# Where VectorE's low parts, two weight sums and the reloads of late sums stand in the projections of a hybrid attention step

## Chip, cores and metric

The kernel runs on one core of a Trainium2 chip. The metric is the device time of one execution in microseconds (us). Before the change the median of three runs is 974.46 us (973.89 to 976.30). Five engines work from queues of their own: TensorE (PE in the profile; PEld are its weight loads), VectorE (DVE), ScalarE (ACT), GpSimd (POOL) and SyncE (SP), which only issues transfers.

## The reference, cut to what matters

One layer of a streaming encoder: RMS norm of x (1024 prompt rows and 64 sample rows, 1024 columns), one projection to 6144 columns, two attention branches (stick-breaking and chunk-band), a merge and an output projection.

```python
def project(x, norm_w, w_in, q_norm_w, k_norm_w):
    h = rms_norm(x, norm_w) @ w_in
    sb_q, sb_k, sb_v, sb_z, cb_q, cb_k, cb_v, cb_z, g_sb, g_cb = jnp.split(h, SPLIT_POINTS, axis=-1)
    ...
    cb_q = rms_norm(cb_q.reshape(lead + (N_HEADS_CB, HEAD_DIM)), q_norm_w)
    cb_k = rms_norm(cb_k.reshape(lead + (N_HEADS_CB, HEAD_DIM)), k_norm_w)
```

The change touches only the first quarter of the execution: the norm of x, and the projections to `cb_q`, `cb_k` and the two value blocks `sb_v` (columns 1024 to 1535) and `cb_v` (3072 to 3583).

## The kernel before

**High and low parts.** All operands are 32-bit floats. TensorE takes them in a reduced format, so each operand is split into a high part (a ScalarE copy that rounds) and a low part (the operand less its high part, one subtraction on VectorE or GpSimd). A product is three matmuls: high by high, low by high, high by low. For x the parts are `xhl`, for weights `whi`/`wlo` (from pool `wpool`) and `whix`/`wlox` (from `natx`), two buffers each. The low part's subtraction reads the high part, so it waits for ScalarE.

**Stage one, steps 0 to 223.** The row blocks of x are normed while the first two weight blocks are already multiplied. `early(at)` is called before each matmul and does the work listed for that step: `prep_s` (L302: square and row sum on ScalarE, then two small GpSimd operations), `prep_a` (L311: scaling on VectorE, at the steps in `SCALE`), `prep_b` (L321 to L330: eight transposes on TensorE, high part on ScalarE, low part on VectorE, at the steps in `READY`), and `W.split` (L134 high, L141 low) of the next weights. The row blocks come in the order `QO`: 0, 1, 2, 3, 8 (the sample rows), 4, 5, 6, 7.

**Passes over `cb_q` and `cb_k`.** For each of the blocks i = 2 to 5 nine row blocks (`ti` 0 to 8) are multiplied (L560), their head norms are taken (`evac_nat` L373 to L376 with two GpSimd operations, `norm_nat` L385), and three or four tiles later they are transposed and stored (`post_nat`: L408 on TensorE, L412 ScalarE, L413 VectorE, then stores). Between the tiles `make_t` builds sums of x: four combinations t0 to t3 of four slices each, in a hand-written order of `yield`s. t0 and t1 are made in these passes, and each slice of t1's unsplit sum is stored to DRAM (`d_t1`).

**The value products.** `sb_v` (j = 0) and `cb_v` (j = 1) are computed by a scheme that trades multiplications for sums: seven products of quarters, numbered s = 0 to 6, instead of eight. Their order is `ORDER`: (0,1), (0,2), (0,6), (0,0), (1,2), (1,1), (1,6), (0,4), (1,0), (1,4), (1,5), (0,5). The position in that list is q, and (q, n) with n = 0 to 3 is one quarter of a product: `part((q, n))` issues the other engines' work, then follow twelve matmuls (L820). Products with s = 0 are two short groups of sample rows only (L710). The weights are quarters of 512 rows and 256 columns, `quad[j, h, w]` (`load_quad`, L510), sums of them (`sum_w`, L440, kept in `made`), and their splits (`split_quad`: L518 high part, L519 low part). Product (0,4) needs all of t2, products (1,5) and (0,5) all of t3. Every second quarter an eviction (`evac_p`) adds a PSUM bank to a sum in SBUF: L726 for partial sums, L729 for a finished block, which `put_v` then stores. Banks are named in `BANKS`: (0,4) writes bank 3 after (1,2), whose result is read at the eviction of (1,1); (1,5) goes on adding to the banks of (1,4) once their eviction has read them.

**Late sums of x.** The second half of `make_t` makes t2 and t3, one slice per call at the quarters in `TJ`: reload the slice of `d_t1` (L211), two VectorE operations (L220, L221 for t2; L223, L224 for t3), then the split `put_t` (L175 high, L176 low), all in one go. The reload of the next slice is issued when a slice is begun; the tiles `d` have two buffers.

**What sets the order.** Each engine takes its instructions in the order in which this program issues them; the order is written out by hand (`manual_schedule`), and a helper adds the semaphore waits that the data needs. Nearly all transfers are issued by SP, in one queue, so a transfer that waits for a buffer holds those behind it.

Of the kernel before, what the change touches and what calls it, by code (L numbers as in the profile page):

```python
# [27 lines left out]
HF = T // 2  # L28
# [6 lines left out]
def hybrid_step_kernel(ctx: ExitStack, tc: tile.TileContext, x_prompt, x_sample, c_sbk, c_sbv, c_cbk, c_cbv,  # L35
# [141 lines left out]

    def make_t(tm, pool):
# [28 lines left out]
        got = {}  # L207

        def fetch(n, k):
            got[n, k] = pool.tile([128, HF], F32, name="d")  # L210
            SP.dma_start(got[n, k], d_t1[k])  # L211

        fetch(*late[0])
        yield
        for e, (n, k) in enumerate(late):
            d = got[n, k]
            if e < 7:
                fetch(*late[e + 1])
# [6 lines left out]
            put_t([t(n, s, k) for s in range(2)], d)  # L225
            yield

    psF = ctx.enter_context(tc.tile_pool(name="af", bufs=2, space=PS))
    with ExitStack() as ph:
# [275 lines left out]
        quad, comb, made = {}, {}, {}  # L505
# [6 lines left out]
        def split_quad(q, src, eng=None):  # L512
# [6 lines left out]
            (eng or G).tensor_tensor(out=l, in0=src, in1=h.bitcast(F32), op=OP.subtract)  # L519
# [42 lines left out]
        SCALE = [24, 48, 72, 96, 122, 148, 174]  # L562
        READY = [12, 36, 60, 84, 110, 136, 162, 190]

        def early(at):
# [60 lines left out]
        for i in range(2, nb):  # L626
# [4 lines left out]
            for ti, t in enumerate(TO):  # L631
# [56 lines left out]
        psB = nu = rw = ws = None  # L688
# [29 lines left out]
        TJ = [(0, 2), (1, 1), (2, 3), (4, 2), (5, 0), (6, 2), (7, 0), (7, 3), (9, 0)]  # L718
        BANKS = {0: "2", 2: "1", 4: "3", 5: "2", 6: "1", 7: "3", 9: "2"}
        u, banks = {(0, "2"): s1t[0]}, {}  # L720
# [11 lines left out]
        def part(at):  # L732
            nonlocal psB, nu, rw, ws, raw1
            if at[0] == 0:
                post_nat(*pend.pop(0))
            if at == (0, 0):
                split_quad(3, quad[0, 0, 1])
# [3 lines left out]
            elif at == (0, 2):  # L741
                sum_w(quad[0, 1, 0], quad[0, 1, 0], made[2], OP.subtract)
                u[0, "3"] = pn.tile([128, 4, 256], F32, name="made2", bufs=1)
# [1148 lines left out]
```

## Time and profile before

| What | Value |
|---|---|
| Median of three runs | 974.46 us (973.89 to 976.30) |
| The profiled execution | 975.09 us |
| Its span, first to last instruction | 973.2 us |
| TensorE busy | 950.6 us, 98% |
| VectorE busy | 595.6 us, 61% |
| ScalarE busy | 498.7 us, 51% |
| GpSimd busy | 382.4 us, 39% |
| Mean granted TensorE clock | 0.993 of full speed |
| Stage one / passes over q and k / value products | 10 to 51 us / 51 to 157 us / 157 to 234 us |

Rows of the order of time read: start in us from the span's start, duration in us, engine, line, operation, output tile <- input tiles, sizes, count, and in brackets the engine's idle time just before and what ended it. Rows of the waits read: engine, tile and line that waited <- the operation waited for, total us, times, longest. A wait for several things is put down to the one that came last in the profile.

### The profile page before, as it was taken

To read this page: it belongs to the slowest core of one execution; us is meant where nothing else is said; L and a number is where in the kernel's file an instruction comes from. 1 tells how busy PE (TensorE), PEld (TensorE's weight loads), DVE (VectorE), ACT (ScalarE), POOL (GpSimd) and SP (SyncE) were. 2 spreads that over 40 slices of the span, in tenths; PEclk is the share of its full clock that TensorE was granted. 3 is DMA by queue.
4 is the path that set the end of the run, shared out by engine and by line. 5 is a ranking of instruction groups with operands and counts; after the bars stand their busy time and mean duration, and the time that the engine had idled before them with its cause. 6 is when DMAs were issued, how large, how long until landed. Compare 5 with 4: busy or idle time off the path is not lost.

```text
span 973.2 us, 20499 instructions
## 1 busy us (share of the span) xinstructions
PE 950.6 (98%) x7547; PEld 903.8 (93%) x7547; DVE 595.6 (61%) x1172; ACT 498.7 (51%) x1151; POOL 382.4 (39%) x387
## 2 busy tenths in 40 slices
PE   8899999959999999999999999999999999999998
PEld 8899999959999999999999987878888888999998
DVE  6746866773554564543332197778678765499735
ACT  7656776222434433433332276667787775466220
POOL 3156664003644465665542201002331111586641
PEclk9999999979999999999999999999999999999999
DMA  7638666455556555565432997779699942862632
GB/s 257 212 128 294 216 241 229 162 165 185 171 178 183 157 166 183 164 192 165 140 116 80 269 259 195 182 202 248 208 297 263 244 126 76 250 204 69 219 126 87
DMA packets 177705, 182.78 MB, mean 188 GB/s; under 512 B 30713, under 2 KB 160125, under 8 KB 177478
## 3 DMA queue, kind: packets, MB, share of 16 engines
q1 hardware_dynamic: 166182, 166.60, 57.3%
q10 hardware_dynamic: 8608, 8.20, 2.6%
q0 software_dynamic: 2816, 6.69, 2.2%
q8 instruction: 60, 0.98, 0.4%
q14 instruction: 39, 0.32, 0.1%
HBM read 117.79 MB, written 63.64 MB: 186 GB/s over the span
## 4 chain that ended last, share of the span: by engine, by line
PE 71%; DMA 3%; ACT 2%; DVE 2%; issue 1%; SPq 1%; ACTq 0%; DVEq 0%
PE b L952 30%; PE o L1474 7%; PE z L1377 7%; PE pt L1430 7%; PE b L1799 6%; PE acc L1228 5%; PE b L1270 5%; PE acc L1121 2%; PE b L820 1%; DMA sq<-d_qsbT 1%; DMA ks<-d_ksbT 1%; PE acc L1842 1%; DVE acc L1315 0%; DMA d<-d_t 0%; PE acc L878 0%
## 5 line engine op out<-in xcount | busy, mean ns | idle before, releaser
L1430 PE MATMUL pt<-ident,be 128*128 128x128 f32 (+1 forms) x568 | 87.1, 277 | 0.9 <-ACT wT L1439 0.6
L1399 DVE TENSOR_TENSOR_SCAN be<-be,imp 128x128 f32<-128x128 f32 (+7 forms) x64 | 82.7, 1341 | 8.3 <-ACT be L1380 8.3
L1377 PE MATMUL z<-ks,sq 128*128 128x320 f32 (+5 forms) x384 | 87.7, 338 | 0.0
L1439 ACT ACTIVATE wT<-pt 128x512 f32<-128x512 f32 (+3 forms) x123 | 57.2, 498 | 44.0 <-PE pt L1430 43.9
L1430 PEld LDWEIGHTS pt<-ident,be 128*128 128x128 f32 (+1 forms) x568 | 66.2, 140 | 13.7 <-issue 5.1
L952 PE MATMUL b<-xm,wlox 128*128 128x256 f32 (+1 forms) x336 | 76.0, 286 | 0.0
L960 DVE TENSOR_TENSOR u<-b,s 128x256 f32<-128x256 f32 (+1 forms) x56 | 24.1, 439 | 70.6 <-PE b L952 68.7
L1377 PEld LDWEIGHTS z<-ks,sq 128*128 128x128 f32 x384 | 63.5, 190 | 2.2 <-ACT be L1380 0.9
L1474 PE MATMUL o<-wT,vp 128*64 128x256 f32 (+1 forms) x608 | 64.2, 357 | 0.0
L1474 PEld LDWEIGHTS o<-wT,vp 128*64 128x64 f32 x608 | 40.3, 137 | 22.4 <-issue 5.4
L952 PEld LDWEIGHTS b<-xm,wlox 128*128 128x128 f32 x336 | 56.8, 188 | 0.0
L1402 ACT ACTIVATE be<-be,sm 128x640 f32<-128x640 f32 (+5 forms) x68 | 47.2, 694 | 17.8 <-DVE sm L1401 17.5
L500 POOL TENSOR_TENSOR whix<-ws,whix 128x512 fp32r<-128x512 f32 x28 | 36.9, 1319 | 36.3 <-ACT whix L499 32.7
L1025 POOL DMA_DIRECT2D d_osb<-zt x20 | 10.8, 541 | 100.8 <-DVE zt L1488 49.2
L1380 ACT ACTIVATE be<-z 128x384 f32<-128x384 f32 (+6 forms) x104 | 48.2, 521 | 3.4 <-PE z L1377 2.9
L500 POOL TENSOR_TENSOR wlo<-ws,wlo 128x512 fp32r<-128x512 f32 x28 | 39.4, 1406 | 26.3 <-ACT wlo L499 24.7
L1390 ACT ACTIVATE be<-be,sm 128x640 f32<-128x640 f32 (+5 forms) x68 | 47.3, 695 | 3.8 <-DVE sm L1382 3.3
L1270 PE MATMUL b<-og,whi 128*128 128x384 f32 (+1 forms) x192 | 46.7, 327 | 0.0
L854 ACT ACTIVATE hl<-u 128x256 f32<-128x256 f32 (+1 forms) x40 | 16.9, 432 | 55.8 <-DVE u L972 17.7
L952 PE MATMUL b<-t0h,whix 128*128 128x256 f32 (+1 forms) x224 | 44.7, 289 | 0.0
L952 PE MATMUL b<-t3h,whi 128*128 128x256 f32 (+1 forms) x224 | 44.6, 289 | 0.0
L385 ACT ACTIVATE qn<-qn,rsn 128x64 f32<-128x64 f32 (+1 forms) x144 | 38.2, 339 | 11.3 <-POOL rsn L293 10.6
(440 smaller groups left out, 3304.6 us busy)
## 6 DMA issues: line engine op xcount, KB each, us to landing
wraw<-in_w_in_dram SPq DMA_DIRECT2D x34, 512.0 KB, 4.6
wrawx<-in_w_in_dram SPq DMA_DIRECT2D x16, 512.0 KB, 3.9
sq<-d_qsbT SPq DMA_DIRECT2D x32, 192.0 KB, 4.8
sq<-d_qcbT SPq DMA_DIRECT2D x32, 192.0 KB, 5.0
xt<-in_x_prompt_dram SPq DMA_DIRECT2D x8, 512.0 KB, 4.7
d_kcbT<-hl SPq DMA_DIRECT2D x8, 512.0 KB
d_qcbT<-hl SPq DMA_DIRECT2D x8, 512.0 KB, 5.0
d_ksbT<-hl SPq DMA_DIRECT2D x16, 256.0 KB, 3.2
```

The source lines that it names most:

```text
L500: G.tensor_tensor(out=t[:, 1], in0=src, in1=t[:, 0].bitcast(F32), op=OP.subtract)
L952: TE.matmul(ps[:, :m], w[:, hl_, k], right[s](x)[:, k, a:b], start=s < 3 and k == 0 and e == 0, stop=k == 3 and e == 2, skip_group_check=s ...
L1228: TE.matmul(ps[:, :e - a], w[:, p, cw], g[:, a:e], start=m % 12 == 0, stop=m % 12 == 11)
L1270: TE.matmul(pp[uu][:, :n], w[:, p, uu * 128:uu * 128 + 128], g[:, a:e], start=p == 0 and m == 0, stop=p == NPAIR - 1 and m == 2)
L1377: TE.matmul(z[:, :m], s[:, e, q0:q0 + 128], ks[:, h, o + x:o + y], start=(e, h) == parts[0], stop=(e, h) == parts[-1])
L1380: A.activation(be[:r, x:y], z[:r, :m], AF.Sigmoid, scale=-0.125)
L1390: A.activation(be[:, :n], be[:, :n], AF.Exp, bias=kp[:, j:j + 1], scale=-1.0, accum_out=kp[:, 2:3])
L1399: V.tensor_tensor_scan(be[:r, n - 1::-1], be[:r, n - 1::-1], im[:, ::-1], 0.0, op0=OP.mult, op1=OP.max)
L1430: TE.transpose(pt[:kr, x, :r], be[:r, kb * 128:kb * 128 + kr], ident[:r, :r])
L1439: A.activation(w[:, sl:sl + m, q0:q0 + r], pt[:, :m, :r], AF.Copy)
L1474: TE.matmul(o[hd * 64:hd * 64 + 64, c0:c1], vv[:kr, kb, hd * 64:hd * 64 + 64], wT[b, p, j, hd, s // 4][:kr, s % 4, c0:c1] if j < 4 else wT ...
L1799: TE.matmul(ps[:, t], left[s](xs_, k)[:, ts_], wt_[:, k], start=s < 3 and t == k == e == 0, stop=k == 3 and e == 2, skip_group_check=s > 2 ...
```

## The change

It has four parts.

1. Low parts. `split_quad` and the late sums no longer issue the low part's subtraction directly behind the high part. They append it to a list `lows`, which `put_lows` empties at the start of the next quarter product (in the last pass: after the next tile's norm). Quads 0 and 3 stay on GpSimd; quad 11's low part goes from GpSimd to VectorE.
2. Weight sums. The sums of `quad[0,0,0]` and of `quad[0,1,0]` move from quarters (0,3) and (0,2) into the last pass, to `ti` 6 and 8; for that `quad[0,1,0]` is loaded earlier, into the buffer where `quad[1,1,1]` was, and that one later. Several sums and splits in the later quarters move by one quarter.
3. Late sums of x. The first two reloads are issued together at quarter (0,1); the first slice's two VectorE operations run at (0,3), its split at (1,0). From (1,2) on two more buffers (`dl`, in a new pool `nd`) take reloads, so a reload is issued two slices ahead or more. The quarters in `TJ` are new.
4. Stage one. Two squares (`prep_s`) go from steps 60 and 84 to 66 and 92, one scaling from step 96 to 86, and the splits of weight block 2 from steps 166 and 200 to 178 and 202.

```diff
+    lows = []
+
+    def put_lows():
+        while lows:
+            eng, lo, src, hi = lows.pop(0)
+            eng.tensor_tensor(out=lo, in0=src, in1=hi.bitcast(F32), op=OP.subtract)
...
-        fetch(*late[0])
-        yield
+        fetch()
+        fetch()
+        nu = yield
         for e, (n, k) in enumerate(late):
-            d = got[n, k]
-            if e < 7:
-                fetch(*late[e + 1])
+            d = got[e]
+            if nu and len(got) < 4:
+                fetch(nu, "dl")
+                fetch(nu, "dl")
+            elif nu and len(got) < 8:
+                fetch(*((nu, "dl") if len(got) > 5 else ()))
...
-            put_t([t(n, s, k) for s in range(2)], d)
-            yield
+            if e == 0:
+                nu = yield
+            hi, lo = (t(n, s, k) for s in range(2))
+            A.activation(hi, d, AF.Copy)
+            lows.append((V, lo, d, hi))
+            nu = yield
...
-        def split_quad(q, src, eng=None):
+        def split_quad(q, src, eng=V):
...
-            (eng or G).tensor_tensor(out=l, in0=src, in1=h.bitcast(F32), op=OP.subtract)
+            lows.append((eng, l, src, h))
...
-        SCALE = [24, 48, 72, 96, 122, 148, 174]
+        SCALE = [24, 48, 72, 86, 122, 148, 174]
...
-                if p + 2 < 9:
+                if p + 2 < 9 and p not in (3, 4):
                     prep_s(QO[p + 2])
+            elif at in (66, 92):
+                prep_s(QO[5 + at // 92])
...
-            elif at == 166:
+            elif at == 178:
                 W.split((2, 0), V)
...
-            elif at == 200:
+            elif at == 202:
                 W.split((2, 1), V)
...
+                put_lows()
                 if (i, ti) == (nb - 1, 2):
...
-                    load_quad(1, 1, 1, wpool, "wraw", 2)
+                    load_quad(0, 1, 0, wpool, "wraw", 2)
...
-                    split_quad(0, made[2])
+                    split_quad(0, made[2], G)
+                if (i, ti) == (nb - 1, 6):
+                    sum_w(quad[0, 0, 0], quad[0, 0, 0], quad[0, 0, 1], OP.subtract)
                 if (i, ti) == (nb - 1, 7):
-                    split_quad(1, made[1], V)
-                    load_quad(0, 1, 0, pn, "made1", 1)
+                    split_quad(1, made[1])
+                if (i, ti) == (nb - 1, 8):
+                    load_quad(1, 1, 1, pn, "made1", 1)
+                    sum_w(quad[0, 1, 0], quad[0, 1, 0], made[2], OP.subtract)
...
-        TJ = [(0, 2), (1, 1), (2, 3), (4, 2), (5, 0), (6, 2), (7, 0), (7, 3), (9, 0)]
+        TJ = [(0, 1), (0, 3), (1, 0), (1, 2), (2, 3), (4, 2), (6, 2), (7, 0), (7, 2), (9, 0)]
...
         def part(at):
+            put_lows()
...
             elif at == (0, 2):
-                sum_w(quad[0, 1, 0], quad[0, 1, 0], made[2], OP.subtract)
...
-            elif at == (0, 3):
-                sum_w(quad[0, 0, 0], quad[0, 0, 0], quad[0, 0, 1], OP.subtract)
                 load_quad(1, 0, 1, wpool, "wraw", 2)
+                split_quad(2, quad[0, 1, 0])
...
-                split_quad(2, quad[0, 1, 0], V)
-            elif at == (1, 2):
+            elif at == (1, 1):
...
+                nd = ndx.enter_context(tc.tile_pool(name="nd", bufs=2))
+                for n in "23":
+                    u[1, n] = nd.tile([128, 4, 256], F32, name="u" + n, bufs=1)
...
             if at in TJ:
-                next(tjobs)
+                tjobs.send(nd)
```

More of the change, by code (lines that the diff above doesn't have):

```diff
@@ L206, in make_t, with fetch @@
         late = [(n, k) for n in (2, 3) for k in range(4)]
[L207 to L211, printed above, removed]
-        fetch(*late[0])
-        yield
-        for e, (n, k) in enumerate(late):
-            d = got[n, k]
-            if e < 7:
-                fetch(*late[e + 1])
+        got = []
+        def fetch(ds=None, name="d"):
+            got.append((ds or pool).tile([128, HF], F32, name=name, bufs=2))
+            SP.dma_start(got[-1], d_t1[late[len(got) - 1][1]])
+        fetch()
+        fetch()
+        nu = yield
+        for e, (n, k) in enumerate(late):
+            d = got[e]
[4 more added lines that the diff above has]
+                fetch(*((nu, "dl") if len(got) > 5 else ()))
             if n == 2:
@@ L503, in prep @@
                 load_raw(2 * i + 4)
-        quad, comb, made = {}, {}, {}
+        quad, comb, made, u = {}, {}, {}, {}
         def load_quad(j, h, w, pool, name, bufs):
@@ L666, in hybrid_step_kernel @@
                 if (i, ti) == (nb - 1, 5):
-                    split_quad(0, made[2])
+                    split_quad(0, made[2], G)
+                if (i, ti) == (nb - 1, 6):
+                    sum_w(quad[0, 0, 0], quad[0, 0, 0], quad[0, 0, 1], OP.subtract)
                 if (i, ti) == (nb - 1, 7):
-                    split_quad(1, made[1], V)
-                    load_quad(0, 1, 0, pn, "made1", 1)
+                    split_quad(1, made[1])
+                if (i, ti) == (nb - 1, 8):
+                    load_quad(1, 1, 1, pn, "made1", 1)
+                    sum_w(quad[0, 1, 0], quad[0, 1, 0], made[2], OP.subtract)
+                    u[0, "3"] = pn.tile([128, 4, 256], F32, name="made2", bufs=1)
                 if (i, ti) in jobs_at:
@@ L686, in hybrid_step_kernel @@
                     V.tensor_scalar(wqk[:, 0], wqk[:, 0], -0.125, None, op0=OP.mult)
-        psB = nu = rw = ws = None
+        psB = nu = nd = rw = ws = None
         def bank_of(b, c):
@@ L732, in part @@
         def part(at):
-            nonlocal psB, nu, rw, ws, raw1
+            nonlocal psB, nu, nd, rw, ws
+            put_lows()
             if at[0] == 0:
@@ L736, in part @@
             if at == (0, 0):
-                split_quad(3, quad[0, 0, 1])
+                split_quad(3, quad[0, 0, 1], G)
+                put_lows()
             elif at == (0, 1):
@@ L759, in part @@
                 nu = ph.enter_context(tc.tile_pool(name="nu", bufs=2))
-                u[1, "2"] = nu.tile([128, 4, 256], F32, name="u2", bufs=1)
+                nd = ndx.enter_context(tc.tile_pool(name="nd", bufs=2))
+                for n in "23":
+                    u[1, n] = nd.tile([128, 4, 256], F32, name="u" + n, bufs=1)
                 SP.dma_start(u[1, "2"][:].rearrange("p t n -> p (t n)"), d_s1)
-                u[1, "3"] = pn.tile([128, 4, 256], F32, name="made1", bufs=1)
             elif at == (1, 3):
@@ L766, in part @@
                 sum_w(made[1], quad[1, 0, 1], quad[1, 1, 1], OP.add)
-                split_quad(4, made[1], V)
+                split_quad(4, made[1])
             elif at == (2, 1):
                 sum_w(made[2], made[1], quad[1, 0, 0], OP.subtract)
-            elif at == (2, 2):
-                split_quad(5, made[2], V)
+                split_quad(5, made[2])
             elif at == (4, 0):
                 sum_w(quad[1, 1, 0], quad[1, 1, 0], made[2], OP.subtract)
-            elif at == (4, 1):
-                split_quad(6, quad[1, 1, 0], V)
+                split_quad(6, quad[1, 1, 0])
             elif at == (5, 1):
-                split_quad(7, quad[0, 0, 0], V)
+                split_quad(7, quad[0, 0, 0])
             elif at == (5, 3):
@@ L783, in part @@
                 open_t((3,))
-                split_quad(8, quad[1, 0, 1], V)
-            elif at == (6, 3):
-                split_quad(9, made[3], V)
-            elif at == (7, 1):
-                split_quad(10, quad[1, 1, 1], V)
+                split_quad(8, quad[1, 0, 1])
+            elif at == (6, 2):
+                split_quad(9, made[3])
+            elif at == (7, 0):
+                split_quad(10, quad[1, 1, 1])
                 load_quad(0, 1, 1, wpool, "wraw", 2)
-            elif at == (7, 2):
+            elif at == (7, 3):
                 load_raw(0)
@@ L793, in part @@
                 split_quad(11, quad[0, 1, 1])
+            elif at == (9, 2):
                 load_raw(1)
@@ L798, in part @@
             elif at == (11, 0):
+                ndx.close()
                 ws = sx.enter_context(tc.tile_pool(name="ws", bufs=3, side="right"))
```

5 lines of the change are left out of this document (2 added, 3 removed).

## Prediction

> **What bounds the kernel now.** I read the page first, then the list of waits, then TensorE's own order of time, and last the two queues that feed it.
>
> ```profile
> span 973.2 us, 20499 instructions
> PE 950.6 (98%) x7547; PEld 903.8 (93%) x7547; DVE 595.6 (61%) x1172; ACT 498.7 (51%) x1151; POOL 382.4 (39%) x387
> ```
> ```profile
> PE b L820 <- ACT wlox L499: 9.2, 1, 9.2
> PE pt L321 <- DVE xn L311: 4.6, 4, 2.5
> PE b L820 <- issue: 2.2, 1, 2.2
> ```
> TensorE sets the end: whatever it does not wait for is hidden. Its waits are 16 us in three places, and the change touches all three. The releasers of L820 are misnamed (ScalarE and "issue"), so I looked at what each product needs.
>
> ```profile
> 195.57 0.55 PE L820 MATMUL b<-whix,t2h 128*128 128x256 f32 x1 [2.18 <-issue]
> 218.87 0.55 PE L820 MATMUL b<-whi,t3h 128*128 128x256 f32 x1 [9.22 <-ACT wlox L499]
> ```
> ```profile
> 190.00:200.00 10.00, 7.82 (x54) 7.64 (x54) 8.95 (x12) 2.56 (x3) 0.00 (x0) 0.83 0.11 30
> 210.00:220.00 10.00, 1.13 (x5) 1.16 (x6) 5.45 (x9) 2.78 (x4) 1.57 (x1) 0.63 0.57 188
> 220.00:230.00 10.00, 10.00 (x76) 10.00 (x75) 0.69 (x1) 0.00 (x0) 2.05 (x2) 0.86 0.68 211
> ```
> Columns of the windows: length, then busy time of PE, PE loads, DVE, ACT, POOL, then granted clock, DMA share, GB/s. The clock falls around both gaps. A mean of 0.83 over 10 us is 3.4 us at half clock (0.17 x 10 / 0.5), at most 1.7 us of matmuls lost; behind the second gap it is 1.1 to the stretch's end and 2.8 in the next (0.14 x 10 / 0.5), at most 1.9 lost.
>
> ```profile
> 178.66 1.23 DVE L519 TENSOR_TENSOR wlox<-r,whix 128x1024 fp32r<-128x1024 f32 x1 [0.59 <-ACT whix L518]
> 179.81 0.72 DVE L220 TENSOR_TENSOR d<-d,xa 128x544 f32<-128x544 f32 x1
> 180.56 0.73 DVE L221 TENSOR_TENSOR d<-d,xm 128x544 f32<-128x544 f32 x1
> 182.01 0.73 DVE L176 TENSOR_TENSOR t2l<-d,t2h 128x544 fp32r<-128x544 f32 x1 [0.72 <-ACT t2h L175]
> 182.65 0.68 DVE L729 TENSOR_TENSOR o<-b,made 128x512 f32<-128x512 f32 x1
> 183.25 1.22 DVE L440 TENSOR_TENSOR r<-r,r 128x1024 f32<-128x1024 f32 x1
> 185.68 1.23 DVE L519 TENSOR_TENSOR wlo<-r,whi 128x1024 fp32r<-128x1024 f32 x1 [1.21 <-ACT whi L518]
> ...
> 194.68 0.69 DVE L726 TENSOR_TENSOR made<-b,u 128x512 f32<-128x512 f32 x1
> ...
> 215.24 0.73 DVE L223 TENSOR_TENSOR d<-xm,d 128x544 f32<-128x544 f32 x1 [2.40 <-DMA d<-d_t]
> ...
> 218.09 1.28 DVE L729 TENSOR_TENSOR o<-b,made 128x512 f32<-128x512 f32 x2
> ```
> So both gaps are VectorE's. The product that starts at 195.57 (0,4) needs bank b3, which the add at 194.68 (ending 195.37) frees. The one at 218.87 (1,5) adds onto the bank that the first eviction at 218.09 has just read. VectorE takes its queue in order, so it hangs wherever a low part stands directly behind its high part: 0.72 us for a part of x, 1.21 for a weight; and 2.40 on the last reload. Before a late eviction comes all of that, summed.
>
> **The change, part by part.** I keep the times of before ("clock of before") and shift at the end.
>
> First stage.
>
> ```profile
> 21.59 1.07 ACT L302 ACTIVATE sq<-xt 128x1024 f32<-128x1024 f32 x1 [0.41 <-DMA xt<-in_x_prompt_dram]
> 22.65 1.04 ACT L134 ACTIVATE whi<-wraw 128x1024 fp32r<-128x1024 f32 x1
> ```
> ```profile
> 23.73 1.22 DVE L141 TENSOR_TENSOR wlo<-wraw,whi 128x1024 fp32r<-128x1024 f32 x1 [1.72 <-ACT whi L134]
> 24.87 1.40 DVE L311 SCALAR_TENSOR_TENSOR xn<-xt,rs,nw 64x512 f32<-64x512 f32 x2
> ...
> 29.29 1.23 DVE L141 TENSOR_TENSOR wlox<-wrawx,whix 128x1024 fp32r<-128x1024 f32 x1 [1.57 <-ACT whix L134]
> ...
> 41.96 1.23 DVE L141 TENSOR_TENSOR wlo<-wraw,whi 128x1024 fp32r<-128x1024 f32 x1
> ```
> ```profile
> 25.75 0.43 PE L321 MATMUL pt<-ident,xn 64*128 64x64 f32 x4 [2.52 <-DVE xn L311]
> ...
> 31.32 1.29 PE L321 MATMUL pt<-ident,xn 128*128 128x128 f32 x8 [1.31 <-DVE xn L311]
> ...
> 43.99 1.29 PE L321 MATMUL pt<-ident,xn 128*128 128x128 f32 x8 [0.51 <-DVE xn L311]
> ```
> - At step 60 the square of the next row block waits for its load until 21.59 and holds the weight's high part behind it. Moved to step 66 it lets the high part start at 21.18 (21.59 less 0.41), 1.47 before 22.65. VectorE is free at 22.01 (23.73 less 1.72), so low part, scaling and transposes all come 1.47 earlier: of 2.52 there stays 1.05. The square then runs at 22.2, 0.6 after its data came; its scaling is wanted from step 86 on, about 26.
> - The scaling of step 96 goes to step 86, ahead of the low part at 29.29. It then follows the sample's parts, at about 27.7 on VectorE, and has its first half by 28.5, before TensorE comes at 30.0 (31.32 less 1.31): 1.31 saved. The second moved square (step 84 to 92) was one more load ahead of that high part.
> - The split of step 166 goes to step 178, behind the scaling: this one starts at 41.96 instead of 43.10, done 43.4, when TensorE comes at 43.48 (43.99 less 0.51): 0.51 saved.
>
> Sum 1.47 + 1.31 + 0.51 = **3.3 us**. From below nothing (the order of ScalarE's queue takes it back), from above all 4.6. I take 3.3 because each step has its row. The two splits (12 and 2 steps later) are covered by the stage's rest, the product that reads them starts after step 224.
>
> The two weight sums.
>
> ```profile
> 159.62 0.41 DVE L413 TENSOR_TENSOR hl<-pt,hl 128x256 fp32r<-128x256 f32 x1
> ...
> 163.09 1.51 DVE L440 TENSOR_TENSOR made<-made,made 128x1024 f32<-128x1024 f32 x1
> 164.52 0.41 DVE L413 TENSOR_TENSOR hl<-pt,hl 128x256 fp32r<-128x256 f32 x1
> 164.85 1.21 DVE L440 TENSOR_TENSOR wrawx<-wrawx,wraw 128x1024 f32<-128x1024 f32 x1
> ```
> ```profile
> 160.76 0.38 PE L408 MATMUL pt<-ident,qn 128*128 128x128 f32 x2
> ```
> Both leave VectorE's queue in the first product for the last norms' tiles. The second (1.21) falls into idle time there. The first now stands with the low part of quad 1 ahead of the eviction at 159.62: the last norm's two operations end near 159.0, low part 1.14, sum 1.14, so that eviction starts at 161.3 and ends at 161.7. The transposes at 160.76 reuse its PSUM tile (two buffers), so TensorE gets a **new wait of 1.1**. It is no cost by itself: TensorE waits longer for VectorE at (1,5) anyway; without that wait it would be 1.1 of loss.
>
> ```profile
> 161.11 2.41 POOL L519 TENSOR_TENSOR wlo<-wraw,whi 128x1024 fp32r<-128x1024 f32 x1
> ```
> The 1.51 beside 1.21 stands while GpSimd subtracts (161.11 to 163.52). The Trainium skill, "SBUF — State Buffer", section "Who interferes with whom", says that a VectorE operation with both inputs in SBUF and a reading GpSimd operation exclude each other; the trace agrees in direction (0.30 longer). By it the moved sum would take 1.21 in its new place and without it 1.51: 0.3 us of queue.
>
> GpSimd's low part of quad 0 now queues behind one more norm (about 2.5 us later, ending near 157.6); its first reader is the third matmul of product (0,1), 157.9: covered, by 0.3 only.
>
> VectorE's queue from 161.3 to the eviction that frees (1,5). Prices are spacings of the rows above: low part 1.15 (178.66 to 179.81), sums of a part of x 0.75 and 0.65, its low part 0.64, eviction add 0.60, weight sum 1.14, post eviction 0.33 (164.52 to 164.85).
> 4 post evictions 1.3; 15 adds 9.0; 8 low parts of weights (quads 2, 4 to 10) 9.2; 4 weight sums 4.6; 8 late parts of x at 2.04, 16.3. Together 40.4.
> Waits that stay, by the new order:
> - four low parts of x (the second and fourth of the first sum, the last two of the second) have nothing between them and their sums, because a quarter without an eviction holds nothing else: 4 x 0.8 (180.56 to 182.01 less 0.65) = 3.2; two have an add between, 0.2 each; two have a weight's low part between, none. Sum 3.6.
> - weights: one directly behind its sum 1.29, two with an add between 0.67 each, the others split a source ready long before. Sum 2.6.
> - at the start 0.9 for ScalarE (last post, quad 2), and for the first reload:
>
> ```profile
> 162.52 1.24 SPq L211 DMA_DIRECT2D d<-d_t x1
> ...
> 210.89 0.55 SPq L211 DMA_DIRECT2D d<-d_t x1
> ```
> ```profile
> 164.00:170.00 6.00, 6.00 (x53) 6.00 (x52) 5.16 (x7) 1.72 (x2) 0.00 (x0) 1.00 0.95 317
> ```
> SP issues it as before near 162.5, behind four stores and a 512 KB load that now waits for quad 1's low part. The last reload needed 4.35 (210.89 to 215.24) when the DMA was less busy; here, at a share of 0.95, it lands near 166.5 to 167, while VectorE now wants it at 165.3 (161.3 + four posts 1.3 + add 0.6 + low part 1.15 + the 0.9): I take 1.1, from 0 to 5.
>
> End: 161.3 + 40.4 + 3.6 + 2.6 + 0.9 + 1.1 = 209.9, with 0.3 for the last add's end and the release 210.2 instead of 218.87: **8.7 us**. TensorE loses its first gap (the add that frees b3 ends near 191 by the same count, wanted at 193.4 + 1.1 = 194.5). It comes to (1,5) after the same work as before, 209.65 (218.87 less 9.22) - 195.57 - 1.5 for the half clock = 12.6, at 207.1. So about 3.1 of waiting stays, and I leave the slow matmuls behind it as they were. Bounds: reload 4 later, 4.7; no wait left, 218.87 - 207.1 = 11.8.
>
> The other edits cost nothing that ends anything: reloads stay eight, the last is issued at quarter (7,0) instead of (7,3), about 5 us before its reader, which removes the 2.40; their buffers and the second sums come from a new pool in space that the norms left; loads of two weight quarters swap places; quad 11's low part goes from GpSimd to VectorE (1.15, behind the add that releases (1,5), so it delays only the next add, 1.7 before that bank is wanted).
>
> Sum 3.3 + 8.7 = 12.0. The profiled execution took 975.09 (span 973.2), 0.63 above the median of 974.46. 975.09 - 12.0 = 963.1 for it, **962.5** for the median.
>
> **Rivals.**
> 1. The first reload, and with it VectorE's queue, is 4 us later: gain 3.3 + 4.7 = 8.0, 966.5. For it: DMA share 0.95. Against: the same reload before had landed by 167.72 without a wait.
> 2. More comes: the queue's waits are hidden and TensorE never waits at (1,5): 11.8 + 3.3 + slow matmuls 1.9 = 17.0, 957.5. Against: 40.4 us of work alone from 161.3 ends at 201.7, so the 8.2 us of waits would have to shrink below 5, and the clock stay up.
> 3. A 3 us wait leaves the clock alone: 1.9 better, 960.6. Against: after only 2.18 idle the 10 us stretch shows 0.83. The Trainium skill, "TensorE: Matmul & The Clock Gate", Part 1, has the clock fall after at least one idle window of about 3.4 us; the trace disagrees, the gap of 2.18 was enough.
> 4. Slower: the first reload is queued so deep that VectorE's whole queue hangs on it. Place: quarter (0,3), where its sum now stands ahead of every eviction and low part. Price: each us of landing past 166.5 goes through to (1,5). Twelve us later, from a landing at 178.5, the change loses; at 181 it is 977.0. For it: SP is in order, and four stores and a 512 KB load stand ahead.
>
> ```profile
> d_qcbT<-hl SPq DMA_DIRECT2D x8, 512.0 KB, 5.0
> ```
> Against: with two of these stores at 512 KB that is some 1.7 MB, 5.4 us at 317 GB/s.
> 5. It doesn't do what it says: the low parts wait as before because too little stands between (true of four of eight), and only the first stage gains: 971.2.
>
> **How the numbers follow.** Forecast 0.62; rival 1 0.13; 2 0.04; 3 0.07; 4 0.06; 5 0.05; nothing at all 0.03. The range runs from 958.5 (forecast, clock untouched, and all 4.6 of the first stage, less 1) to 968.5 (rival 1 without part of the first stage). Faster by over 0.3% (2.9 us, about what a measurement here can tell) 0.90, within 0.04, slower 0.06.
>
> **What would show it.** TensorE's wait on VectorE's scaling near 1.3 in all instead of 4.6; a new wait of about 1 at L408's transposes for VectorE; no gap ahead of (0,4); a gap of about 3 ahead of (1,5), with the clock low after it; no wait of VectorE on the last reload, about 1 on the first. I am wrong if (1,5)'s gap stays over 6 or a gap opens in the first products.

## The result, and the profile after

The changed kernel takes **963.81 us** (median of four runs, 963.69 to 965.89) where the kernel before takes 974.22 (four runs, 973.89 to 976.30): a ratio of 0.9894, 95% interval 0.9874 to 0.9913, or 10.4 us less. The profiled execution took 965.89 with a span of 964.0; the spans of the other three were 961.8 to 962.0. Measured again later, the same two kernels gave 964.00 (five runs, 963.02 to 964.24) and 976.52 (974.14 to 978.92), ratio 0.9873 (0.9854 to 0.9892), 12.5 us less. In both the interval lies below 1: the kernel is faster, by a little over 1%. The forecast of 962.5 lies within 1.5 us of either median.

The page of the kernel after, span and engines:

```profile
span 964.0 us, 20499 instructions
PE 950.3 (99%) x7547; PEld 904.2 (94%) x7547; DVE 597.9 (62%) x1173; ACT 498.7 (52%) x1151; POOL 384.8 (40%) x386
```

TensorE's work is what it was (950.3 us against 950.6). What went is waiting. The list of waits, kernel after, TensorE's rows from the places the change touches:

```profile
PE b L842 <- ACT wlox L514: 4.4, 1, 4.4
...
PE pt L336 <- DVE xn L326: 1.3, 3, 0.9
...
PE pt L423 <- DVE hl L428: 0.6, 1, 0.6
PE b L842 <- POOL wlo L183: 0.2, 1, 0.2
```

Against 9.2, 2.2 and 4.6 before: the 2.2 is gone, 4.4 is left ahead of product (1,5) and 1.3 in the first stage, and 0.6 and 0.2 are new. TensorE's order of time, kernel after, shows the instructions that waited, and at 28.27 the group of transposes that waited 1.31 before and has no wait now:

```profile
24.17 0.43 PE L336 MATMUL pt<-ident,xn 64*128 64x64 f32 x4 [0.94 <-DVE xn L326]
24.84 0.43 PE L336 MATMUL pt<-ident,xn 64*128 64x64 f32 x4 [0.23 <-DVE xn L326]
...
28.27 1.03 PE L336 MATMUL pt<-ident,xn 128*128 128x128 f32 x8
...
157.80 0.44 PE L423 MATMUL pt<-ident,qn 128*128 128x128 f32 x2 [0.64 <-DVE hl L428]
...
207.12 0.55 PE L842 MATMUL b<-whi,t3h 128*128 128x256 f32 x1 [4.38 <-ACT wlox L514]
```

As before, "ACT wlox" names the wrong releaser. VectorE's order of time, kernel after, gives the right one:

```profile
156.19 1.22 DVE L455 TENSOR_TENSOR wraw<-wraw,made 128x1024 f32<-128x1024 f32 x1
157.33 0.41 DVE L428 TENSOR_TENSOR hl<-pt,hl 128x256 fp32r<-128x256 f32 x1
...
162.71 0.73 DVE L231 TENSOR_TENSOR d<-d,xa 128x544 f32<-128x544 f32 x1 [0.52 <-DMA d<-d_t]
...
181.76 1.23 DVE L183 TENSOR_TENSOR wlo<-r,whi 128x1024 fp32r<-128x1024 f32 x1 [1.21 <-ACT whi L533]
...
185.10 0.73 DVE L183 TENSOR_TENSOR t2l<-dl,t2h 128x544 fp32r<-128x544 f32 x1 [0.72 <-ACT t2h L239]
...
187.07 1.22 DVE L183 TENSOR_TENSOR wlox<-wrawx,whix 128x1024 fp32r<-128x1024 f32 x1
188.32 1.22 DVE L455 TENSOR_TENSOR wrawx<-r,wraw 128x1024 f32<-128x1024 f32 x1
...
202.25 0.73 DVE L183 TENSOR_TENSOR t3l<-dl,t3h 128x544 fp32r<-128x544 f32 x1 [0.73 <-ACT t3h L239]
...
205.69 0.72 DVE L183 TENSOR_TENSOR t3l<-dl,t3h 128x544 fp32r<-128x544 f32 x1 [0.72 <-ACT t3h L239]
206.33 0.68 DVE L752 TENSOR_TENSOR o<-b,u 128x512 f32<-128x512 f32 x1
```

The add at 206.33 empties the bank that (1,5) adds onto; it ends at 207.01 and TensorE goes on at 207.12, where it went on at 218.87 before: 11.75 us earlier. The weight's low part at 187.07 comes one quarter behind its high part and has no wait; those of x at 185.10, 202.25 and 205.69 have no other work between them and their sums and still wait 0.72. The last reload's 2.40 is gone; the first one costs 0.52.

### The profile page after: what moved, and what is told of

Its sections match the earlier page's. It is cut to its first block, busy times and chain, and to the rows that moved or that the text cites. A ratio compares the mean times of both kernels' runs of the same rounds, so it can differ in the third digit from the quotient of the medians.

```text
span 964.0 us, 20499 instructions
## 1 busy us (share of the span) xinstructions
PE 950.3 (99%) x7547; PEld 904.2 (94%) x7547; DVE 597.9 (62%) x1173; ACT 498.7 (52%) x1151; POOL 384.8 (40%) x386
## 4 chain that ended last, share of the span: by engine, by line
PE 82%; DVE 7%; DMA 4%; ACT 2%; issue 2%; POOL 1%; SPq 1%; DVEq 0%; ACTq 0%; POOLq 0%
PE b L974 30%; PE acc L575 11%; PE o L1496 7%; PE z L1399 7%; PE pt L1452 7%; PE b L1821 6%; PE acc L1250 5%; PE b L1292 2%; PE acc L1143 2%; PE b L842 1%; DVE acc L1337 1%; DMA vs<-d_dv 1%; PE b L575 1%; DVE tk L1334 1%; PE pt L336 1%
## 5 line engine op out<-in xcount | busy, mean ns | idle before, releaser
L515 POOL TENSOR_TENSOR wlox<-wraw,wlox 128x512 fp32r<-128x512 f32 x19 | 28.2, 1484 | 75.0 <-ACT wlox L514 75.0
```

The source lines that it names most:

```text
L515: G.tensor_tensor(out=t[:, 1], in0=src, in1=t[:, 0].bitcast(F32), op=OP.subtract)
```

## The experiments

They ran in four batches, each beside its own runs of the kernel before (medians 975.75 for the first four kernels, 976.38 for the next four, 976.09 for the two behind these, 976.52 for the last), so ratios and places in the profile are compared, not bare times. The kernel after ran beside the last batch only: "after" as a control is its 0.9873, with the gap of 4.4 above (4.9 in the profile of that second measurement). Next to the gap ahead of (1,5) I give the start of the stage that follows the value products: 233.9 before, 222.9 after in both profiles. "The release" is VectorE's add that empties the bank (1,5) adds onto; it starts at 206.33 in the kernel after.

**Stage one alone**: the kernel before with part 4 of the change.

```diff
-        SCALE = [24, 48, 72, 96, 122, 148, 174]
+        SCALE = [24, 48, 72, 86, 122, 148, 174]
...
+            elif at in (66, 92):
+                prep_s(QO[5 + at // 92])
...
-            elif at == 166:
+            elif at == 178:
```

> The kernel before with only the edits of stage one. Theory (the scaling on VectorE is late because the high part on ScalarE and the low part stand ahead of it): TensorE's wait on the scaling falls from 4.6 to 1.3 us as in the whole change, the two gaps of the value products stay at 2.2 and 9.2, and the time falls by 3.3, to about 971. Rival (the value products are bound by transfers at fixed times, so an earlier TensorE only waits longer there): the same shorter wait in stage one, but the gap of 9.2 grows to about 12 and the time stays at 974.

Measured: 971.78 against 975.75, ratio 0.9955 (0.9942 to 0.9968), 4.0 us less. The list of waits of this kernel, TensorE:

```profile
PE b L822 <- ACT wlox L499: 9.7, 1, 9.7
PE b L822 <- issue: 2.4, 1, 2.4
PE pt L321 <- DVE xn L311: 1.4, 3, 1.0
```

The stage's waits fall by 3.2, near the 3.3 of the forecast (4.6 to 1.4), and the gaps of the value products do not take it back: they are 9.7 and 2.4 long where they were 9.2 and 2.2. (This profiled execution itself took 973.52, the longest of its eight; it ran 3.4 us of the first stage at half clock, which the last section comes back to.)

**The value products alone**: the kernel after with the first stage of before.

```diff
-        SCALE = [24, 48, 72, 86, 122, 148, 174]
+        SCALE = [24, 48, 72, 96, 122, 148, 174]
...
-                if p + 2 < 9 and p not in (3, 4):
+                if p + 2 < 9:
```

> The whole change without the edits of stage one. Theory (the two stages add): TensorE's wait on the scaling is 4.6 again, one gap of about 4.4 is left ahead of product (1,5), and the time is 3.3 above the changed kernel: 967. Rival (the earlier start of the value products is itself needed, or wasted, there): anything else than 966 to 968.

Measured: 968.09, ratio 0.9917 (0.9894 to 0.9940), 7.7 us less than 975.75; gap ahead of (1,5) 4.6, first-stage waits 4.5. 4.0 + 7.7 = 11.7 lies between the 10.4 and the 12.5 that the whole change gained: as far as these intervals tell, the two halves add up.

**Low parts at once**: the kernel after, with the list emptied directly behind each high part. Quad 11's low part, which the kernel before had on GpSimd and the kernel after has on VectorE behind the release, then stands on VectorE ahead of the release.

```diff
             lows.append((V, lo, d, hi))
+            put_lows()
...
             lows.append((eng, l, src, h))
+            put_lows()
```

> The whole change, but each low part is issued directly behind its high part again. Theory (VectorE's in-order queue pays 0.7 for a late part of x and 1.2 for a weight whose source was just made): the waits that come back are about 0.6 each for quads 4 and 5, 0.6 each for the first and third slice of t2, 0.8 each for the first two slices of t3, 0.5 elsewhere, some 4.5 to 5.3 in all; the gap ahead of (1,5) grows from 4.4 to about 9 and the time to 968.5. Rival (ScalarE is far enough ahead that queueing hides nothing, the gain is the moved sums and the reloads): gap 4.4 to 5.5, time 964 to 965.

Measured: 969.61, ratio 0.9931 (0.9908 to 0.9954). Waits and order of time of this kernel, TensorE and VectorE:

```profile
PE b L844 <- issue: 9.1, 1, 9.1
```
```profile
164.50 0.72 DVE L231 TENSOR_TENSOR d<-d,xa 128x544 f32<-128x544 f32 x1 [1.59 <-DMA d<-d_t]
...
185.12 1.23 DVE L183 TENSOR_TENSOR wlo<-r,whi 128x1024 fp32r<-128x1024 f32 x1 [1.21 <-ACT whi L534]
...
188.47 0.72 DVE L183 TENSOR_TENSOR t2l<-dl,t2h 128x544 fp32r<-128x544 f32 x1 [0.72 <-ACT t2h L239]
189.42 1.23 DVE L183 TENSOR_TENSOR wlox<-wrawx,whix 128x1024 fp32r<-128x1024 f32 x1 [0.22 <-ACT whix L534]
...
191.88 1.22 DVE L456 TENSOR_TENSOR wrawx<-r,wraw 128x1024 f32<-128x1024 f32 x1
...
211.86 1.23 DVE L183 TENSOR_TENSOR wlox<-wraw,whix 128x1024 fp32r<-128x1024 f32 x1 [0.22 <-ACT whix L534]
213.00 1.28 DVE L754 TENSOR_TENSOR o<-b,u 128x512 f32<-128x512 f32 x2
```

The release comes at 213.00, 6.7 us later than in the kernel after (206.33), the gap grows from 4.4 to 9.1 and the next stage starts at 228.5, 5.6 late. Not all of the 6.7 are waits of low parts. 1.8 of it is there at the first slice's sum already (164.50 against 162.71): the first reload is waited for 1.59 in place of 0.52; whether the edit does that, the run does not show. 1.8 more come up to the weight sum at 191.88 (188.32 in the kernel after), and 1.5 behind it, from two low parts of x (0.77 and 0.73) that do not wait in the kernel after; these 3.3 are waits for ScalarE that the held-back order hides. The last 1.4 is quad 11's low part at 211.86, work that stands ahead of the release here and behind it in the kernel after (0.22 of it is a wait). So the expected gap of 9 came, but in part from terms that were not in the expectation. By the ratios (0.9931 less 0.9894 or 0.9873) the whole edit is worth 3.6 to 5.7 us, by the next stage about half of the 11.0 us by which that stage came earlier.

**The two weight sums back** to (0,2) and (0,3), and the load that depends on one of them with it:

```diff
-                if (i, ti) == (nb - 1, 6):
-                    sum_w(quad[0, 0, 0], quad[0, 0, 0], quad[0, 0, 1], OP.subtract)
...
             elif at == (0, 2):
+                sum_w(quad[0, 1, 0], quad[0, 1, 0], made[2], OP.subtract)
...
+            elif at == (0, 3):
+                sum_w(quad[0, 0, 0], quad[0, 0, 0], quad[0, 0, 1], OP.subtract)
```

> The whole change, but the two weight sums are done in quarters (0,2) and (0,3) again, and with them the load of one weight quarter is issued at (0,3). Theory (queue length): the eviction add that releases (1,5) comes later by the two sums, 2.3 us, less up to 0.5 that VectorE idles on the first reload; gap about 6.5, time 965.7 to 966. The new wait at the transposes (0.6) goes. Rival (they fall into idle time in either place): gap 4.4, time 963.5.

Measured: 964.99, ratio 0.9880 (0.9851 to 0.9910), not to be told from after; gap 3.7, and a further 1.7 of waits in the same products; next stage at 224.7. Neither the expected gap of 6.5 nor the expected time came. VectorE's and GpSimd's order of time, this kernel:

```profile
160.27 1.72 DVE L455 TENSOR_TENSOR wraw<-wraw,made 128x1024 f32<-128x1024 f32 x1
...
209.11 0.68 DVE L748 TENSOR_TENSOR o<-b,u 128x512 f32<-128x512 f32 x1
...
158.50 2.41 POOL L183 TENSOR_TENSOR wlo<-wraw,whi 128x1024 fp32r<-128x1024 f32 x1
```

VectorE's queue did get longer as expected: from the first of the last post evictions, which starts at nearly the same time (157.47, in the kernel after 157.33), to the release at 209.11 it takes 2.6 us more. The gap is short because TensorE came to it 3.5 later (209.89 less 3.68 = 206.21, after 202.74): 1.7 are the further waits, and the value products began 1.3 later (154.7 against 153.4), with 3.4 us at half clock in the first stage, as in the kernel with stage one alone. The sum's own price beside GpSimd is 0.5 us: it took 1.72 here, with GpSimd subtracting until 160.91, and 1.22 in its new place (156.19, in the kernel after). What the two moves are worth in the whole stays open: 0.9880 lies between the two ratios measured for the kernel after, 0.9894 and 0.9873.

**Two reload buffers** instead of four, each reload one slice ahead:

```diff
-            if nu and len(got) < 4:
-                fetch(nu, "dl")
-                fetch(nu, "dl")
-            elif nu and len(got) < 8:
-                fetch(*((nu, "dl") if len(got) > 5 else ()))
+            if 0 < e < 7:
+                fetch()
```

> The whole change, but the reloads use two buffers and each is issued one slice ahead (the first two still together). Theory (the reload takes about 4.3 us from its issue, and is now issued one slice, about 3.5 us, ahead of its reader for the last three slices): VectorE waits 0.5 to 2 us on reloads in the last slices, the gap ahead of (1,5) grows by that to 5 to 6.5, time 964.5 to 966. Rival (the queued low parts and moved sums alone are enough, the buffers are not needed): gap 4.4, time within 0.5 of the changed kernel.

Measured: 965.95, ratio 0.9894 (0.9877 to 0.9911); gap 7.1, next stage at 224.6, 1.7 later than after. VectorE's order of time, this kernel:

```profile
162.26 0.72 DVE L228 TENSOR_TENSOR d<-d,xa 128x544 f32<-128x544 f32 x1 [1.04 <-DMA d<-d_t]
...
196.15 0.73 DVE L231 TENSOR_TENSOR d<-xm,d 128x544 f32<-128x544 f32 x1 [0.45 <-DMA d<-d_t]
...
201.63 0.73 DVE L231 TENSOR_TENSOR d<-xm,d 128x544 f32<-128x544 f32 x1 [1.63 <-DMA d<-d_t]
```

With two buffers the late reloads are waited for again, 0.45 + 1.63 = 2.1, and the first one 0.5 longer (1.04 against 0.52), 2.6 in all. The queue began 1.0 earlier in this execution (first post eviction at 156.35, after 157.33), so the release comes 1.6 later (207.92); the rest of the 2.7 by which the gap is longer is TensorE, which came 1.1 earlier (208.70 less 7.05 = 201.65, after 202.74).

**VectorE's queue made longer**: the low parts of quads 9 and 10 are subtracted twice, with the same result.

```diff
-            lows.append((eng, l, src, h))
+            lows.extend([(eng, l, src, h)] * (2 if q in (9, 10) else 1))
```

> The whole change with the low parts of quads 9 and 10 subtracted twice on VectorE (the same values written again). Theory (VectorE's queue sets the start of product (1,5)): every added us goes through, 2 x 1.14 = 2.3 us, gap 6.7, time 966 to 966.5. Rival (the start of (1,5) is set by the last reload or by ScalarE): gap 4.4 to 5, time within 0.7 of the changed kernel.

Measured: 965.41, ratio 0.9890 (0.9872 to 0.9907); gap 7.2, next stage at 225.1. VectorE, this kernel:

```profile
194.92 2.48 DVE L183 TENSOR_TENSOR wlox<-wrawx,whix 128x1024 fp32r<-128x1024 f32 x2
...
199.94 2.48 DVE L183 TENSOR_TENSOR wlo<-made,whi 128x1024 fp32r<-128x1024 f32 x2
...
209.85 0.68 DVE L752 TENSOR_TENSOR o<-b,u 128x512 f32<-128x512 f32 x1
```

From each doubled subtraction to the operation behind it 2.40 us pass (194.92 to 197.32, 199.94 to 202.34), 1.14 and 1.13 in the kernel after, so 2.5 us are added. The release starts 3.5 later (209.85 against 206.33): 1.0 was there ahead of the first doubled one (194.92 against 193.91), in an execution that waited 0.76 us more in the first stage, and the added 2.5 went through one to one. So the gap of 4.4 is set by VectorE's queue, not by the last reload or by ScalarE's last high part. That the next stage starts 2.2 later, about the length of the two subtractions, is chance: the half clock ended near 213.8 here, 3.1 us behind TensorE's restart at 210.64, and 5.7 us behind it in the kernel after.

**Less on VectorE**: the low parts of quads 8, 9 and 10 on GpSimd, which has no work between 180 and 200 us in the kernel after.

```diff
-                split_quad(8, quad[1, 0, 1])
+                split_quad(8, quad[1, 0, 1], G)
```

> The whole change with the low parts of quads 8, 9 and 10 on GpSimd instead of VectorE (2.4 us each there, GpSimd is idle at that time). Theory by queue length: VectorE is shorter by 3 x 1.14 = 3.4, the gap falls from 4.4 to about 1, no half clock behind it, time 959 to 960.5. Rival (a VectorE operation with two inputs in SBUF and a GpSimd operation that reads SBUF exclude each other): the sums of x and low parts that meet GpSimd get longer by up to the 2.4 they meet, up to 7 in all, so the gap falls by less than 2 or grows, and durations of L231 to L235 above 0.72 show it; time 962.5 to 967.

Measured: 967.03, ratio 0.9912 (0.9895 to 0.9930); gap 8.5, next stage at 227.1, 4.2 **later**. GpSimd and VectorE, order of time of this kernel:

```profile
187.16 2.41 POOL L183 TENSOR_TENSOR wlo<-wraw,whi 128x1024 fp32r<-128x1024 f32 x1 [26.65 <-ACT whi L533]
193.17 2.40 POOL L183 TENSOR_TENSOR wlox<-wrawx,whix 128x1024 fp32r<-128x1024 f32 x1 [3.60 <-ACT whix L533]
198.73 2.40 POOL L183 TENSOR_TENSOR wlo<-made,whi 128x1024 fp32r<-128x1024 f32 x1 [3.16 <-ACT whi L533]
```
```profile
187.19 3.46 DVE L183 TENSOR_TENSOR wlox<-wrawx,whix 128x1024 fp32r<-128x1024 f32 x1
...
193.15 0.68 DVE L752 TENSOR_TENSOR o<-b,u 128x512 f32<-128x512 f32 x1
193.75 2.39 DVE L234 TENSOR_TENSOR d<-xm,d 128x544 f32<-128x544 f32 x1
...
197.68 0.72 DVE L183 TENSOR_TENSOR t3l<-d,t3h 128x544 fp32r<-128x544 f32 x1 [0.78 <-ACT t3h L239]
...
198.92 2.78 DVE L234 TENSOR_TENSOR d<-xm,d 128x544 f32<-128x544 f32 x1
...
203.19 0.72 DVE L183 TENSOR_TENSOR t3l<-d,t3h 128x544 fp32r<-128x544 f32 x1 [0.72 <-ACT t3h L239]
```

Three subtractions of 1.14 leave VectorE (3.4 us), and three operations beside GpSimd's grow from 1.22 to 3.46, from 0.72 to 2.39 and from 0.72 to 2.78, by 6.0 together. The add at 193.15, one of whose inputs is in PSUM, keeps its 0.68 although GpSimd's second subtraction runs over it. The Trainium skill, "SBUF — State Buffer", section "Who interferes with whom", says that a VectorE instruction with two SBUF inputs contends with a GpSimd instruction that reads SBUF, and calls the port pair they share an exclusive lock; the trace agrees: the three stretched operations end 1.08, 0.57 and 0.57 us behind the end of GpSimd's (190.65 less 189.57, 196.14 less 195.57, 201.70 less 201.13), nearly their own length of 1.22, 0.72 and 0.72, as if they had begun only then, and the add with an input in PSUM goes through.

The edit also took away cover. In the kernel after a weight's low part stands between the sums of x and their low part at 195.05 and at 198.81, and neither waits; here the same two wait 0.78 and 0.72 (197.68 and 203.19). 6.0 + 1.5 - 3.4 = 4.1 is nearly the 4.4 by which the release comes later (210.71 against 206.33).

**The scaling first in stage one**: the split of weight block (1,0) in two, its high part at step 62, its low part at step 74 behind the scaling.

```diff
             elif at == 62:
-                W.split((1, 0), V)
+                W.hi((1, 0))
+            elif at == 74:
+                W.lo((1, 0), V)
                 load_nat(2, 0)
```

> The whole change, and in stage one the low part of weight block 1's first half (and the load behind it) goes from step 62 to step 74, behind the scaling of the sample rows at step 72; its high part stays. Theory: the 1.2 us that TensorE still waits for that scaling go to about 0.2, nothing else waits, time 962.6. Rival (the low part is then late for its first product at step 92, or the load behind it for block 2): a new wait of 0.5 or more on the weights, time 963.5 or more.

Measured: 962.05, ratio 0.9853 (0.9837 to 0.9868), which is 2.0 us below after's 0.9873. First-stage waits 0.2 in place of 1.3, gap 4.3, next stage at 220.7, 2.2 earlier. More came than the 1.1 of the wait. In this profile the release is 1.1 earlier (205.27), and the rest lies behind the gap, where the half clock lasted 3.4 us instead of 6.8, which nothing in the edit is known to set. Two of the other three runs (962.05 and 962.25) have the mean clock of the kernel after, 0.996, so where the rest comes from in them stays open.

**The waited-for slice last**: the kernel of the last experiment, with the last two slices of the late sum, quad 11 and two loads moved by one to three quarters and product (1,5) reordered: all four of its quarters take the first three slices of the late sum, and only then the fourth.

```diff
+            if q == 10:
+                for ks in (range(3), range(3, 4)):
+                    for c in range(2):
+                        ps = banks[j, 4, c]
+                        for tt in range(2):
+                            if ks[0] == 0:
+                                part((q, 2 * c + tt))
+                            for k in ks:
...
```

> The kernel with the scaling first in stage one, and ahead of product (1,5): the last slice's job goes from quarter (9,0) to (9,3), behind the eviction add that releases the bank, the one before it from (7,2) to (7,3) so that an add stands between it and its low part, quad 11's split one quarter later, and product (1,5) takes slices 0 to 2 of all four quarters first and slice 3 last. Theory (the gap is the place of one add in VectorE's queue, not the length of the queue): the release comes 3 to 4 us earlier, the gap falls from 4.3 to 0.5 to 1.5, no half clock follows, and the time is 3.5 to 5 below the kernel with the scaling first, 1.9% below the kernel before. Rival (the wait only moves on, to the first products of the next stage, which need sums that stand behind evictions that wait for stores): the gap falls as said, but a new wait of 1.5 to 3 opens at the next stage's second product, and the time falls by 2 or less.

Measured: 959.33, ratio 0.9825 (0.9805 to 0.9846); next stage at 218.4. TensorE and VectorE, order of time of this kernel:

```profile
203.22 0.36 PE L844 MATMUL b<-whi,t3h 128*128 128x256 f32 x1 [2.23 <-issue]
```
```profile
202.42 0.69 DVE L754 TENSOR_TENSOR o<-b,u 128x512 f32<-128x512 f32 x1 [1.11 <-DMA out_dram<-o]
```

The gap fell from 4.3 to 2.2, less than expected. The add that ends it now waits itself, 1.11, for a store to leave one of the two `o` blocks: with the queue before it shortened, the blocks are late next.

**The fold of the sample rows later**: in this kernel, the last operation of (1,5) put behind the first sums of the product that follows.

```diff
-            if h:
+            if h and put:
                 put_s(j, 1, fold(nu.tile([128, 512], F32, name="o")[0:64], ps))
...
+                    if q == 11 and c == tt == 0:
+                        put_s(1, 1, fold(nu.tile([128, 512], F32, name="o")[0:64], made["a", 1]))
```

> The same, and the sample rows' result of cb_v is folded behind the next stage's first sums instead of ahead of them. If the wait moved on to the next stage, this takes 0.5 to 1 us of it back; if not, it is the same as the one before within 0.5.

Measured: 960.35, ratio 0.9833 (0.9812 to 0.9854), no gain. From the start of the value products to the next stage it takes 66.7 us (152.8 to 219.5), the kernel before this one 66.9 (151.5 to 218.4). The gap is 2.0, and behind it TensorE waits 1.9 for the second add, which itself waits 1.04 for a store to leave an `o` block (0.85 in the kernel before this one). The order of the folds does not bind; whether the blocks do is what the next kernel tests.

**A block of its own**: in the kernel with slice 3 last (the fold is where it was), product (1,4)'s finished blocks go to a buffer that is free by then, not to the two `o` blocks.

```diff
-            v = nu.tile([128, 512], F32, name="o")
+            if (j, s) == (1, 4):
+                if c == 0:
+                    made["v"] = pn.tile([128, 4, 256], F32, name="made1", bufs=1)
+                v = two(made["v"])
+            else:
+                v = nu.tile([128, 512], F32, name="o")[:]
```

> The kernel with slice 3 last, and the two finished blocks of product (1,4) go to a free buffer of their own instead of the two blocks that still wait for their stores. Theory (the 2.2 us still ahead of (1,5) are an add that waits 1.1 for a store, behind VectorE's queue): the add comes about 1 us earlier, the gap falls to about 1, the later evictions and the fold no longer wait 4.8 for stores, and the time is 1 to 2 below the kernel with slice 3 last (ratio about 0.981). Rival (TensorE's gap is then set by the queue alone, as before the store's wait): gap 1.7 to 2.2, time the same within 0.5.

> The changed kernel itself once more, on the same chip as the kernel beside it, as the measure for the single edits: ratio 0.987 to 0.991 to the kernel before, gap ahead of (1,5) 4.4.

Measured: **957.28**, ratio 0.9808 (0.9788 to 0.9827); the kernel after beside it 964.00, so 6.7 us below it. TensorE's and VectorE's order of time, this kernel:

```profile
201.99 0.35 PE L849 MATMUL b<-whi,t3h 128*128 128x256 f32 x1 [0.86 <-ACT whix L533]
205.07 0.38 PE L849 MATMUL b<-whi,t3h 128*128 128x256 f32 x1 [0.72 <-DVE made L759]
```
```profile
201.20 0.68 DVE L759 TENSOR_TENSOR made<-b,u 128x512 f32<-128x512 f32 x1
```

The add comes at 201.20 without a wait, TensorE waits 0.86 and 0.72 in place of 4.4, the clock is 1.00 in every 5 us stretch from 205 to 240, and the next stage starts at 216.1, 6.8 before the kernel after: the 6.7 of the measurement. Against the kernel with slice 3 last the intervals of the ratios overlap (0.9808 and 0.9825); the release is 1.2 earlier, as expected, and that kernel had 3.4 us of half clock here, worth up to 1.7, which this one has not. One part of the expectation failed: a later add, at 208.10, still waits 2.24 for a store, and the fold, at 214.11, follows a wait of 4.64 (4.76 in the kernel with slice 3 last). It is the fastest kernel of these experiments.

## Why the prediction was right, point by point

**What bounds.** Right: the value products run at VectorE's pace. Doubling two of its operations delayed the release by what was added, and shortening the path in front of the add gave it back.

**First stage, 3.3.** Right in its steps, 1.47 + 1.31 + 0.51, and 0.9 too small. The second and third wait are gone, the first is 0.94 where 1.05 was left. But the value products begin at 153.4 where they began at 157.6, 4.2 earlier. The two groups of transposes that no longer wait also run shorter, 1.03 and 1.04 us (at 28.27 and 40.01) for 1.29 each, which is 0.5 of the 0.9; what the rest is stays open. Alone the stage gave 4.0 us, with an interval (976 x 0.0032 to 0.0058, 3.1 to 5.7) that holds both.

**The two weight sums.** The post eviction started at 157.33, where 161.3 less 3.3 is 158.0; the new wait was 0.64 for 1.1. GpSimd's low part, "covered by 0.3 only", was late by 0.2. That the sum would keep its 1.22 away from GpSimd was right (1.51 before, 1.72 put back).

**VectorE's queue to the release, 48.6 (209.9 less 161.3).** Measured 49.6, from 157.33 to the add's 206.33 + 0.60. The waits that stay were counted rightly: four of 0.72 where nothing stands between, 1.21, 0.65 and 0.58 for the weights (2.44 for 2.6). The first reload, taken at 1.1 from a range of 0 to 5, cost 0.52; ScalarE at the start cost 0.32 + 0.60 + 0.53 = 1.45 for 0.9. In all the waits are some 0.5 less than summed, so the 40.4 of work was short by some 1.5: the spacings between neighbours that were its prices may leave out small delays elsewhere in the queue.

**The release**: 11.75 earlier for a forecast of 3.3 + 8.7 = 12.0. Part of that closeness is luck: the queue began 0.7 early, its waits were 0.5 less and its work 1.5 more than summed. The gap was 4.4 for "about 3.1", because TensorE came 1.1 earlier (207.12 less 4.38 = 202.74, forecast 207.1 less 3.3 = 203.8), by the 0.9 that the first stage gave beyond its sum; VectorE came only 0.2 later (207.12 for 210.2 less 3.3 = 206.9).

**The step that was mis-sized** is "I leave the slow matmuls behind it as they were". The windows of the kernel after (length, then busy time of PE, PE loads, DVE, ACT, POOL, granted clock, DMA share, GB/s):

```profile
205.00:210.00 5.00, 2.88 (x13) 2.91 (x14) 3.06 (x4) 2.12 (x3) 2.10 (x1) 0.60 0.64 202
210.00:215.00 5.00, 5.00 (x34) 5.00 (x33) 0.69 (x1) 0.00 (x0) 0.00 (x0) 0.72 0.93 280
215.00:220.00 5.00, 5.00 (x45) 5.00 (x45) 2.46 (x5) 0.43 (x2) 0.00 (x0) 1.00 0.42 138
```

Half clock for 4.0 + 2.8 = 6.8 us, that is from about 206.0 to 212.8 (in stretches of 1 us the clock is 1.00 up to 206, 0.50 from there and 0.58 from 212 to 213). The matmuls start at 207.12, so 5.7 us of them are slow and 2.8 are lost, where the prediction read 3.9 us and 1.9 in the kernel before. A stretch of half clock that began later than the idle time reached further past it. So the next stage starts 11.0 earlier (233.9 to 222.9) and not 11.75.

**From 11.0 to the measured 10.4 and 12.5.** The two profiles of the kernel after agree up to the last product (873.7 us in both, 884.7 before); there the first takes until 960.1 for its last matmuls, the second until 957.6 (969.3 before), at a granted clock of 1.00 until 955 in both. The two executions differ by 2.5 us in work that the change does not touch; the cause stays open. The sum of 12.0 lies between what the two measurements show.

**Rivals.** The reload that comes 4 us later, or hangs the whole queue, did not happen (0.52). That the waits stay as before was true of four low parts of x and three of weights, as counted, and false of the rest: low parts at once put 3.3 us of waits back. A wait of 4.4 did not leave the clock alone. That TensorE would no longer wait at (1,5) needed other edits: the last kernel comes near it, with 0.86 + 0.72.

## What to carry to other kernels

In an engine that takes its queue in order, an operation that depends on another engine's last result belongs one block of independent work later: here that hid some 3.3 us of waits without one operation saved. Find the one eviction that releases the bound engine, sum the queue in front of it, and then ask what that eviction itself needs, since with the queue shortened its output block was late next (the add waited 1.11 for it, and nothing with a block of its own). An engine that sits idle is no free place for work that shares an SBUF port with the bound one: taking 3.4 us off VectorE in that way made the next stage 4.2 us later.

## What the runs showed of the hardware that was not expected

**Half clock comes in multiples of 3.4 us, and whether a short wait brings it depends on the execution.** Windows of two kernels with the same first stage; the kernel with stage one alone, then the kernel after:

```profile
25.00:30.00 5.00, 5.00 (x30) 4.93 (x31) 3.31 (x5) 2.88 (x7) 1.44 (x2) 0.66 0.72 235
```
```profile
25.00:30.00 5.00, 5.00 (x46) 4.93 (x46) 3.77 (x6) 4.15 (x10) 1.44 (x2) 1.00 0.78 249
```

Both waited 0.94 to 0.96 and 0.23 us just before; one got 3.4 us of half clock (0.34 x 5 / 0.5), 30 matmuls in the stretch for 46, and the other none. The kernel before waited longer at that place, 2.52 and 0.23, and its profile shows 1.00 from 15 to 50 us.

The half clock around the gaps of the value products, summed from the clock in stretches of 1 us, is 3.4, 6.8 or 10.2 us in every one of the 14 cases in the profiles of this document: 3.4 with gaps of 2.2, 2.2, 2.4, 3.7, 4.3 and 4.6 us, 6.8 with 4.4, 4.9 and 7.2, 10.2 with 7.1, 8.5, 9.1, 9.2 and 9.7. There was none with 2.0 and 1.9 (the fold later) or 0.9 and 0.7 (the last kernel). These are multiples of one length, and a gap of 4.4 can bring more than one of 4.6, so the length of the wait alone does not decide. A phase that the kernel does not set could, and it could be why executions of one kernel differ by 1 to 2 us; that is argued, not tested by itself. The Trainium skill, "TensorE: Matmul & The Clock Gate", Part 1, states a free-running window of about 3.4 us, which agrees with the lengths; that the clock falls after at least one idle window of that length does not agree with the gaps of 2.2 us or with 0.96 + 0.23 us of waiting.

**GpSimd can cost VectorE more than it takes over**: 6.0 us of stretched operations for 3.4 us taken off, in the rows of that experiment. The prediction had weighed this at 0.3 us for one operation (1.51 for 1.21), from a pair that overlapped only in part; a whole overlap costs 1.7 to 2.2.
